# Seven block products of a gated FFN: another product order, earlier reading out of PSUM, and later joins of the transposed blocks

## The chip, the cores and the metric

The kernel runs on one NeuronCore of a Trainium2 chip. The metric is the device time of one execution in microseconds (us), the median of several executions. A profiled execution gives, beside its time, a trace of every instruction on five engines: TensorE (PE, the matmuls; PEld, its weight loads), VectorE (DVE), ScalarE (ACT), GpSimd (POOL) and SyncE (SP, which here only issues transfers).

## The reference

A decoder trunk of two layers on 512 tokens of width 1024. Each layer is a half-step SwiGLU, a mixing block of three attention branches, and a second half-step SwiGLU:

```python
def _swiglu(t, w_gate, w_up, w_down):
    return (jax.nn.silu(t @ w_gate) * (t @ w_up)) @ w_down

for l in range(DEPTH):                                    # DEPTH = 2
    f = _swiglu(_rmsnorm(h, ffn1_pre_g[l]), ffn1_w_gate[l], ffn1_w_up[l], ffn1_w_down[l])
    h = h + 0.5 * _rmsnorm(f, ffn1_post_g[l])
    ...                                                   # mixing block
    f = _swiglu(_rmsnorm(h, ffn2_pre_g[l]), ffn2_w_gate[l], ffn2_w_up[l], ffn2_w_down[l])
    h = h + 0.5 * _rmsnorm(f, ffn2_post_g[l])
```

The FFN is 2816 features wide. All is float32, and the change touches only the four FFNs, which the program names a0, c0, a1, c1 (a: first of a layer, c: second).

## The kernel before

**Three matmuls for one.** TensorE multiplies float32 operands as a sum of a rounded high part and a low part. `split` (L182, L183) makes the pair: ACT casts the source to the high part (wh, uh, ah), DVE subtracts it from the source to get the low part (wl, ul, al). `mm3` then issues three matmuls for one product: high by high (L205), high by low weights (L206), low activations by high weights (L207).

**Seven products for eight.** 2048 of the 2816 features of an FFN go through a Strassen-Winograd scheme: the activations are cut into 2 x 2 blocks (halves of the tokens by halves of the 1024 inputs), the weights into 2 x 2 blocks as well, and seven products of sums of blocks stand for eight block products. A run of seven products handles 1024 features of one matrix. So an FFN has four such groups, in this order: G0 and U0 (gate and up, features 0 to 1023), G1 and U1 (gate and up, features 1024 to 2047). Behind them come 14 products of the down projection, D, in the same manner. The remaining 768 features go as plain products, a pair of 128-feature blocks ahead of G0 and the others between the D products.

**One product.** `token_product(ci, up, n, uns)` issues product n of a group: 24 matmuls of 128x512, over two weight units (k0 = 0 and 2) and two PSUM banks e. The seven products use three pairs of banks: c0 collects products 0, 3, 5 and 6, c1 is a copy of c0 made after product 0 (L747, on ACT) onto which product 1 adds, and c2 collects products 2 and 4. After each product but 0 its sum is read out of PSUM into SBUF while the bank goes on collecting: products 2 and 3 by ACT copies (L775), products 4 and 5 by DVE additions (L777, followed by L784 or L786), products 1 and 6 by ACT silu (L781, gate) or DVE multiplication (L779, up). So product 5 may not write into a bank of c0 before product 3 is read out of it, and product 6 not before product 5 is.

**Order.** `ORDER` is 0, 2, 1, 3, 4, 5, 6 for all four groups. `sums` makes the sums of activation blocks (x00, x11 and the pairs uh/ul of products 2 to 5) in steps spread over the first products of G0. `BlockUnit` loads a raw weight block; for products 2, 3, 5, 6 a DVE subtraction (L327) forms the sum of weight blocks, in a kept tile t or in the raw tile; products 2 and 4 inherit raw tiles of products 0 and 3. The raw tiles come in turn from the pools "raw" (2 buffers) and "o".

**Turning the result.** A product of activations by weights has the tokens on the partitions, and the down projection needs the features there. So each finished up block (after products 1, 4, 5, 6) is transposed by `turn`, called behind the matmuls of each later product: two ACT copies (L800) separate its 16-bit halves, SP issues two DMA transposes (L801), and two products later two ACT copies join the halves (L804). The halves land in an own buffer for products 1 and 5, in short-lived tiles for 4 and 6.

**Who sets the order on an engine.** The code is traced once, and a list scheduler orders the instructions of each engine by priority and by its own cost estimates; parts of the program are pinned to the written order, these groups are not. Each engine then runs its list strictly in order, waiting on semaphores. The loads are issued by SP ahead of their use, within the buffers of the pools.

## Time and profile before

| | us |
|---|---|
| runs | 2379.33, 2377.66, 2384.99 (median 2379.33) |
| profiled execution: its time | 2378.89 |
| profiled execution: span | 2377.2 |
| PE busy | 2348.8 |
| DVE busy | 1805.5 |
| ACT busy | 1515.2 |
| POOL busy | 76.0 |
| mean granted TensorE clock | 0.999 |

The span is the time from the first to the last instruction. Matmuls are pipelined: one 128x512 matmul has about 0.39 us in the trace, but the next starts 0.227 us after it, so that a busy PE can't be taken for a PE at its peak; what is lost there is seen in its waits. A row of the timeline gives start, duration, engine, line, operation, output<-input, shape, and in brackets the idle time of the engine ahead of it with what ended it. In the names, pwa0u is a PSUM bank of FFN a0, group "up"; pda one of the down products; wh_ga and wl_ga weights (gate, FFN of kind a), ula the low part of a sum of activation blocks, hra and sa gate and up results in SBUF.

### The profile page before, as it was taken

The numbers are of one execution on the slowest core, as the hardware profiler recorded it, in microseconds if no ns is written. First come the engines' busy times: TensorE is split into PE (matmuls) and PEld (weight loads), VectorE is DVE, ScalarE is ACT, GpSimd is POOL, SyncE is SP. The second block draws the span as 40 slices with busy tenths as digits, with TensorE's granted clock in tenths as the row PEclk, the third lists the DMA queues.
The fourth block names the chain that finished last, engine by engine and source line by source line (L and its number), as shares of the span: only waits on it lengthen the run. The fifth ranks groups of instructions, "written<-read, shape, count | busy, mean of one in ns | idle before, by whom it ended". The sixth has DMA issues, their size and how long they took to land.

```text
span 2377.2 us, 31155 instructions
## 1 busy us (share of the span) xinstructions
PE 2348.8 (99%) x11719; PEld 1982.8 (83%) x11719; DVE 1805.5 (76%) x2358; ACT 1515.2 (64%) x2306; POOL 76.0 (3%) x134
## 2 busy tenths in 40 slices
PE   9999999999999999999999999999999999999998
PEld 7777889888888888778888878888888888887787
DVE  8876877667777689778788778766777767897785
ACT  6777565577766556775557665655777664666744
POOL 0000000000111000000000000000001100000000
PEclk9999999999999999999999999999999999999999
DMA  5666455223223556664647664532323235576643
GB/s 199 194 176 182 159 190 151 75 81 94 86 75 107 186 178 177 185 186 142 230 134 208 182 177 161 199 110 71 98 72 98 80 116 200 160 203 171 194 145 141
DMA packets 299754, 354.98 MB, mean 149 GB/s; under 512 B 78266, under 2 KB 192978, under 8 KB 299604
## 3 DMA queue, kind: packets, MB, share of 16 engines
q1 hardware_dynamic: 299508, 352.97, 48.3%
q8 instruction: 92, 1.51, 0.3%
q14 instruction: 58, 0.48, 0.1%
q0 software_dynamic: 96, 0.03, 0.0%
HBM read 319.39 MB, written 16.78 MB: 141 GB/s over the span
## 4 chain that ended last, share of the span: by engine, by line
PE 84%; DVE 5%; DMA 5%; ACT 4%; issue 2%; SPq 0%; POOL 0%; DVEq 0%; ACTq 0%
PE pg L206 4%; PE pg L205 4%; PE pg L207 4%; PE pda L206 2%; PE pda L207 2%; PE pdc L206 2%; PE pda L205 2%; PE pdc L207 2%; PE pdc L205 2%; PE pb L207 1%; PE pb L206 1%; PE pb L205 1%; DMA raw_da<-in_ffn_w_down_dram 1%; PE pq L206 1%; PE pq L205 1%
## 5 line engine op out<-in xcount | busy, mean ns | idle before, releaser
L205 PE MATMUL pg<-us_a,wh_wg 128*128 128x512 f32 x384 | 150.9, 393 | 0.0
L207 PE MATMUL pg<-us_a,wl_wg 128*128 128x512 f32 x384 | 149.8, 390 | 0.0
L206 PE MATMUL pg<-us_a,wh_wg 128*128 128x512 f32 x384 | 149.8, 390 | 0.0
L206 PE MATMUL pda<-wl_da,aha 128*128 128x512 f32 x224 | 87.8, 392 | 3.5 <-DVE wl_da L183 3.5
L206 PE MATMUL pdc<-wl_dc,ahc 128*128 128x512 f32 x224 | 87.9, 392 | 3.0 <-DVE wl_dc L183 3.0
L205 PE MATMUL pdc<-wh_dc,ahc 128*128 128x512 f32 x224 | 86.8, 390 | 1.4 <-ACT wh_dc L182 1.3
L205 PE MATMUL pda<-wh_da,aha 128*128 128x512 f32 x224 | 86.7, 390 | 1.1 <-ACT wh_da L182 1.1
L207 PE MATMUL pdc<-wh_dc,alc 128*128 128x512 f32 x224 | 87.2, 389 | 0.0
L207 PE MATMUL pda<-wh_da,ala 128*128 128x512 f32 x224 | 87.2, 389 | 0.0
L183 DVE TENSOR_TENSOR wl_da<-raw_da,wh_da 128x1024 fp32r<-128x1024 f32 x50 | 60.9, 1223 | 34.3 <-ACT wh_da L182 34.3
L207 PEld LDWEIGHTS pg<-us_a,wl_wg 128*128 128x128 f32 x384 | 72.1, 188 | 15.2
L183 DVE TENSOR_TENSOR wl_dc<-raw_dc,wh_dc 128x1024 fp32r<-128x1024 f32 x50 | 61.0, 1222 | 30.5 <-ACT wh_dc L182 30.4
L205 PEld LDWEIGHTS pg<-us_a,wh_wg 128*128 128x128 f32 x384 | 72.1, 188 | 14.1
L206 PEld LDWEIGHTS pg<-us_a,wh_wg 128*128 128x128 f32 x384 | 72.2, 188 | 14.1
L182 ACT CAST wh_da<-raw_da 128x1024 fp32r<-128x1024 f32 x50 | 52.2, 1050 | 47.0 <-PE pda L207 16.6
L182 ACT CAST wh_dc<-raw_dc 128x1024 fp32r<-128x1024 f32 x50 | 52.3, 1050 | 43.5 <-PE pdc L207 17.6
L186 DVE SCALAR_TENSOR_TENSOR wl_wg<-raw_wg,wh_wg 128x1024 fp32r<-128x1024 f32 x48 | 58.4, 1220 | 22.2 <-ACT wh_wg L185 22.2
L200 DVE SCALAR_TENSOR_TENSOR ga<-pg,bgate,ga 128x512 f32<-128x512 f32 x48 | 35.9, 747 | 50.0 <-ACT ga L199 50.0
L185 ACT ACTIVATE wh_wg<-raw_wg 128x1024 fp32r<-128x1024 f32 x48 | 50.6, 1058 | 24.7 <-PE pv L1096 11.7
L183 DVE TENSOR_TENSOR wl_uc<-raw_uc,wh_uc 128x1024 fp32r<-128x1024 f32 x44 | 53.7, 1220 | 16.5 <-ACT wh_uc L182 16.5
L182 ACT CAST wh_uc<-raw_uc 128x1024 fp32r<-128x1024 f32 x44 | 46.1, 1050 | 30.7 <-PE pgc L206 7.6
L183 DVE TENSOR_TENSOR wl_ua<-raw_ua,wh_ua 128x1024 fp32r<-128x1024 f32 x44 | 53.6, 1219 | 15.0 <-ACT wh_ua L182 15.0
(647 smaller groups left out, 8053.7 us busy)
## 6 DMA issues: line engine op xcount, KB each, us to landing
raw_da<-in_ffn_w_down_dram SPq DMA_DIRECT2D x66, 512.0 KB, 4.4
raw_dc<-in_ffn_w_down_dram SPq DMA_DIRECT2D x66, 512.0 KB, 4.2
raw_ga<-in_ffn_w_gate_dram SPq DMA_DIRECT2D x52, 512.0 KB, 4.3
raw_ua<-in_ffn_w_up_dram SPq DMA_DIRECT2D x52, 512.0 KB, 4.4
raw_gc<-in_ffn_w_gate_dram SPq DMA_DIRECT2D x52, 512.0 KB, 4.1
raw_uc<-in_ffn_w_up_dram SPq DMA_DIRECT2D x52, 512.0 KB, 3.6
raw_wg<-in_w_gate_dram SPq DMA_DIRECT2D x48, 512.0 KB, 3.5
raw_wo<-in_w_out_dram SPq DMA_DIRECT2D x24, 512.0 KB, 3.4
```

The lines of the kernel that those rows point to most:

```text
L182: both = [nc.scalar.copy(h_ap, src)]
L183: make = lambda: nc.vector.tensor_tensor(l_ap, src, h_ap.bitcast(F32), ALU.subtract)
L185: both = [nc.scalar.activation(h_ap, src, AF.Copy, scale=scale)]
L186: make = lambda: nc.vector.scalar_tensor_tensor(l_ap, src, scale, h_ap.bitcast(F32), ALU.mult, ALU.subtract)
L200: nc.vector.scalar_tensor_tensor(t, z, minus, t, ALU.max, ALU.add)
L205: nc.tensor.matmul(pt, lh, rh, start=start, stop=False, skip_group_check=free)
L206: nc.tensor.matmul(pt, lh, rl, start=False, stop=False, skip_group_check=free)
L207: nc.tensor.matmul(pt, ll, rh, start=False, stop=stop, skip_group_check=free)
```

## The change

The product order is a table by group: G0, U0 and G1 take 0, 2, 3, 1, 5, 4, 6, and U1 keeps 0, 2, 1, 3, 4, 5, 6. Where the raw tile of a product lies is now a table by product instead of a cycle. The copy of c0 into c1 is issued ahead of product 2 instead of ahead of product 1, and the banks of c1 are taken there too. All reading out of PSUM, of the token products and of the down products, is issued under a higher scheduler priority. The halves of a transposed block lie in the own buffer by the position of its product among the four (first and third), and the join comes two products later for the second of the four and, in U0, the first; for the others it comes three products later. The computation and the number of matmuls (11,348 rows on PE) stay the same.

```diff
-    ORDER = (0, 2, 1, 3, 4, 5, 6)
+    ORDERS = ((0, 2, 3, 1, 5, 4, 6), (0, 2, 1, 3, 4, 5, 6))
+    PLACES = ("raw", "o"), ("raw", "o"), (None, None), ("o", "o"), (None, None), ("raw", "o"), ("raw", "o")
...
-            if n in (0, 1, 2):
-                st["c", n] = [pbank("z" if n == 0 else "mm", f"pw{nm}_{e}") for e in range(2)]
-            if n == 1:
+            for c in {0: (0,), 2: (2, 1)}.get(n, ()):
+                st["c", c] = [pbank("mm" if c else "z", f"pw{nm}_{c}{e}") for e in range(2)]
+            if n == 2:
                 for e in range(2):
+                  with tc.high_priority(offset=300):
                     nc.scalar.copy(st["c", 1][e][:], st["c", 0][e][:])
...
+            with tc.high_priority(offset=300):
+                for e in range(2):
+                    p = pts[e][:].rearrange("p (f q) -> p f q", f=2)
...
             if up and n in (1, 4, 5, 6):
-                turns.append([nm, g, (2 * ci + q[1], q[0]), n in (1, 5), 0, None])
+                at = [n for n in ORDERS[ci] if n in (1, 4, 5, 6)].index(n)
+                turns.append([nm, g, (2 * ci + q[1], q[0]), at % 2 == 0, 0, None, 2 if at == 1 or ci == 0 and at == 0 else 3])
...
-                if kk in (0, 1) and age == 2:
+                if kk in (0, 1) and age == back:
...
-            turns[:] = [one for one in turns if one[4] < 3]
+            turns[:] = [one for one in turns if one[4] <= one[6]]
...
-            places, had = itertools.cycle(("raw", "o", "o")), {}
-            for n in ORDER:
-                uns = [BlockUnit(n, w, ND // 2, k, 2, S, keep, f"{nm}_{n}_{k}", n in (2, 4) or next(places))
+            had, order = {}, ORDERS[ci and up]
+            for n in order:
+                uns = [BlockUnit(n, w, ND // 2, k, 2, S, keep, f"{nm}_{n}_{k}", PLACES[n][k // 2])
...
-                early = ci == 0 and not up and n in ORDER[:4]
+                early = ci == 0 and not up and n in order[:4]
...
         def product(at, uns):
...
+            with tc.high_priority(offset=300):
+                if n == 0:
+                    st["b", 1] = [pbank("z", f"pd{name}_1_{e}") for e in range(2)]
```

In the changed file the lines stand lower by 1 (L716 becomes L717, L719 L720), 2 (L747 becomes L749) or 3 (L777 becomes L780, L784 L787); L182, L183 and L327 keep theirs. In the order lists that follow a row is line, operation, output<-inputs and shape. A weight tile such as wl_gc_0_3_0 is the low part for FFN kind c, gate, group 0, product 3, unit 0, with a buffer number behind it.

The first place is DVE in G0 of c0, from the last splits of product 2's surroundings to the low part ulc_3 that product 3 needs. Before:

```order
L183 TENSOR_TENSOR wl_gc_0_1_0_8083<-raw_gc_0_1_0_7933,wh_gc_0_1_0_8082 128x1024
L183 TENSOR_TENSOR hidc_17_8079<-sc_17_8076,hidc_17_8079 128x512
L716 TENSOR_TENSOR x11c_7997<-x11c_7997,x00c_8036 128x1024
L183 TENSOR_TENSOR wl_gc_0_1_2_8089<-raw_gc_0_1_2_7935,wh_gc_0_1_2_8088 128x1024
L327 TENSOR_TENSOR tgc_0_0_7929<-raw_gc_0_3_0_7937,tgc_0_0_7929 128x1024
L183 TENSOR_TENSOR ulc_3_8104<-x11c_7997,uhc_3_8103 128x1024
```

Now, from the same point of the program:

```order
L327 TENSOR_TENSOR tgc_0_0_7929<-raw_gc_0_3_0_7933,tgc_0_0_7929 128x1024
L183 TENSOR_TENSOR hidc_17_8079<-sc_17_8076,hidc_17_8079 128x512
L327 TENSOR_TENSOR tgc_0_2_7931<-raw_gc_0_3_2_7935,tgc_0_2_7931 128x1024
L183 TENSOR_TENSOR wl_gc_0_3_0_8084<-tgc_0_0_7929,wh_gc_0_3_0_8083 128x1024
L717 TENSOR_TENSOR x11c_7997<-x11c_7997,x00c_8036 128x1024
L183 TENSOR_TENSOR wl_gc_0_3_2_8089<-tgc_0_2_7931,wh_gc_0_3_2_8088 128x1024
L183 TENSOR_TENSOR wl_gc_0_1_0_8124<-raw_gc_0_1_0_7937,wh_gc_0_1_0_8123 128x1024
L183 TENSOR_TENSOR ulc_3_8102<-x11c_7997,uhc_3_8101 128x1024
```

Ahead of ulc_3 DVE now has two operations of 128x1024 more than before, and the product that reads ulc_3 comes one product earlier.

The second place is PE in a0, at the end of G1's product 5 (before) or 4 (now) and the beginning of its product 6, whose weights are wh_ga_1_6. Before:

```order
L207 MATMUL pwa0g_0_1_1135<-wh_ga_1_5_2_1268,ula_5_665 128x512
L205 MATMUL pwa0u_0_0_1430<-wh_ua_1_0_0_1342,us_x_130 128x512
L206 MATMUL pwa0u_0_0_1430<-wl_ua_1_0_0_1343,us_x_130 128x512
L205 MATMUL pwa0g_0_0_1134<-wh_ga_1_6_0_1300,us_x_131 128x512
L206 MATMUL pwa0g_0_0_1134<-wl_ga_1_6_0_1301,us_x_131 128x512
```

Now:

```order
L206 MATMUL pwa0g_2_21_1181<-wl_ga_1_4_2_1265,uha_4_623 128x512
L207 MATMUL pwa0g_2_21_1181<-wh_ga_1_4_2_1264,ula_4_624 128x512
L205 MATMUL pwa0g_0_00_1132<-wh_ga_1_6_0_1298,us_x_131 128x512
L206 MATMUL pwa0g_0_00_1132<-wl_ga_1_6_0_1299,us_x_131 128x512
L207 MATMUL pwa0g_0_00_1132<-wh_ga_1_6_0_1298,us_x_131 128x512
```

Two matmuls of U1's product 0 stood ahead of product 6; they now stand behind it, with the rest of their product.

The third place is DVE at the end of U1 in a0, where the down products begin (wl_da_0_0_0 are the low weights of the first). Before:

```order
L183 TENSOR_TENSOR wl_ua_1_6_2_1589<-tua_1_2_1263,wh_ua_1_6_2_1588 128x1024
L183 TENSOR_TENSOR ala_1_0_1739<-hra_2_1531,aha_1_0_1738 128x1024
L183 TENSOR_TENSOR wl_da_0_0_0_1624<-raw_da_0_0_0_1539,wh_da_0_0_0_1623 128x1024
L777 TENSOR_TENSOR hra_3_1492<-hra_3_1492,pwa0u_0_0_1430 128x2x256
L777 TENSOR_TENSOR hra_3_1492<-hra_3_1492,pwa0u_0_1_1431 128x2x256
```

Now:

```order
L183 TENSOR_TENSOR wl_ua_1_6_2_1593<-tua_1_2_1229,wh_ua_1_6_2_1592 128x1024
L183 TENSOR_TENSOR ala_1_0_1739<-hra_2_1531,aha_1_0_1738 128x1024
L780 TENSOR_TENSOR hra_3_1496<-hra_3_1496,pwa0u_0_00_1430 128x2x256
L183 TENSOR_TENSOR wl_da_0_0_0_1624<-raw_da_0_0_0_1539,wh_da_0_0_0_1623 128x1024
L780 TENSOR_TENSOR hra_3_1496<-hra_3_1496,pwa0u_0_01_1431 128x2x256
```

The reading out of product 5's first bank moved ahead of the split of the first down weights. On PE, four matmuls of the first down product stood ahead of U1's product 6 here; they now stand behind it.

More of the change, by code (lines that the diff above doesn't have):

```diff
@@ L770, in token_product @@
             r = hidden_rows(2 * ci + q[1])[:, :, HALVES[q[0]]] if up else g
-            for e in range(2):
-                p = pts[e][:].rearrange("p (f q) -> p f q", f=2)
-                re, ge = r[:, 2 * e:2 * e + 2], g[:, 2 * e:2 * e + 2]
-                if n in (2, 3):
-                    nc.scalar.copy(re, p)
-                elif n in (4, 5):
-                    nc.vector.tensor_tensor(re, re, p, ALU.add)
-                elif up:
-                    nc.vector.tensor_tensor(ge, p, ge, ALU.mult)
-                else:
-                    nc.scalar.activation(re, p, AF.Silu)
-            if n in (4, 5):
-                if up:
-                    nc.vector.tensor_tensor(g, r, g, ALU.mult)
-                else:
-                    nc.scalar.activation(r, r, AF.Silu)
+            with tc.high_priority(offset=300):
+                for e in range(2):
+                    p = pts[e][:].rearrange("p (f q) -> p f q", f=2)
+                    re, ge = r[:, 2 * e:2 * e + 2], g[:, 2 * e:2 * e + 2]
+                    if n in (2, 3):
+                        nc.scalar.copy(re, p)
+                    elif n in (4, 5):
+                        nc.vector.tensor_tensor(re, re, p, ALU.add)
+                    elif up:
+                        nc.vector.tensor_tensor(ge, p, ge, ALU.mult)
+                    else:
+                        nc.scalar.activation(re, p, AF.Silu)
+                if n in (4, 5):
+                    if up:
+                        nc.vector.tensor_tensor(g, r, g, ALU.mult)
+                    else:
+                        nc.scalar.activation(r, r, AF.Silu)
             if up and n in (1, 4, 5, 6):
-                turns.append([nm, g, (2 * ci + q[1], q[0]), n in (1, 5), 0, None])
+                at = [n for n in ORDERS[ci] if n in (1, 4, 5, 6)].index(n)
+                turns.append([nm, g, (2 * ci + q[1], q[0]), at % 2 == 0, 0, None, 2 if at == 1 or ci == 0 and at == 0 else 3])
         def turn(kk):
             for one in turns:
-                nm, g, (row, i), own, age, planes = one
+                nm, g, (row, i), own, age, planes, back = one
                 if kk == 1 and age == 0:
@@ L874, in product @@
                 return
-            if n == 0:
-                st["b", 1] = [pbank("z", f"pd{name}_1_{e}") for e in range(2)]
-                for e in range(2):
-                    nc.scalar.copy(st["b", 1][e][:], pts[e][:])
-                return
-            i, hf = TO[n]
-            for e in range(2):
-                f = dst.fs[2 * i + e][:, HF[hf]]
-                if n in (4, 5):
-                    nc.vector.tensor_tensor(f, f, pts[e][:], ALU.add)
-                else:
-                    nc.scalar.copy(f, pts[e][:])
+            with tc.high_priority(offset=300):
+                if n == 0:
+                    st["b", 1] = [pbank("z", f"pd{name}_1_{e}") for e in range(2)]
+                    for e in range(2):
+                        nc.scalar.copy(st["b", 1][e][:], pts[e][:])
+                    return
+                i, hf = TO[n]
+                for e in range(2):
+                    f = dst.fs[2 * i + e][:, HF[hf]]
+                    if n in (4, 5):
+                        nc.vector.tensor_tensor(f, f, pts[e][:], ALU.add)
+                    else:
+                        nc.scalar.copy(f, pts[e][:])
         def products():
```

## The prediction

> **What bounds the kernel now.** I read the page's head first, then the list of what PE waits for, then the timeline around each of those waits. The head of the page:

> ```profile
> span 2377.2 us, 31155 instructions
> PE 2348.8 (99%) x11719; PEld 1982.8 (83%) x11719; DVE 1805.5 (76%) x2358; ACT 1515.2 (64%) x2306; POOL 76.0 (3%) x134
> ```

> PE is busy in all but 2377.2 - 2348.8 = 28.4 us. The change keeps every matmul, so it can win no more than idle time of PE, and only that in the FFNs. The view of PE's waits (line that waits, what ended the wait: us in all, times, longest) names it:

> ```profile
> PE pda L206 <- DVE wl_da L183: 3.5, 4, 1.3
> PE pdc L206 <- DVE wl_dc L183: 3.0, 4, 0.8
> PE pwa0u L205 <- ACT wh_ga L182: 2.0, 1, 2.0
> ...
> PE pdc L205 <- ACT wh_dc L182: 1.3, 1, 1.3
> PE pda L205 <- ACT wh_da L182: 1.1, 1, 1.1
> PE pwa0g L207 <- DVE ula L183: 1.1, 1, 1.1
> PE pwc1u L206 <- DVE wl_uc L183: 0.8, 1, 0.8
> PE pwa0u L206 <- DVE wl_ua L183: 0.8, 1, 0.8
> ...
> PE pwa1u L206 <- DVE wl_ua L183: 0.6, 1, 0.6
> ...
> PE pwa0u L205 <- ACT wh_ua L182: 0.5, 1, 0.5
> PE pwc1u L205 <- ACT wh_uc L182: 0.5, 1, 0.5
> ...
> PE pwc0u L206 <- DVE wl_uc L183: 0.4, 1, 0.4
> PE pwc0u L205 <- ACT wh_gc L182: 0.3, 1, 0.3
> ```

> By place these are: the two rows of wh_ga and wh_gc, 2.3 us, at product 6 of U0 (a0 and c0); six rows of ua and uc, 0.8 + 0.8 + 0.6 + 0.5 + 0.5 + 0.4 = 3.6 us, at the first matmuls of U1, which stand ahead of G1's product 6; the four rows of da and dc, 3.5 + 3.0 + 1.3 + 1.1 = 8.9 us, in D; and 1.1 us at G0's product 4 in a0. Together 15.9 us, 0.7% of the time. That is the most that can be won, and it needs all of them to go with nothing new.

> **Term 1, product 6 of U0.** The chain in a0, from the timelines of ACT, DVE and PE:

> ```profile
> 108.97 1.36 ACT L804 COPY hra<-tra0u 128x1024 uint16<-128x1024 uint16 x1 [1.78 <-DMA tra0u<-tha0u]
> 110.21 1.03 ACT L182 CAST wh_ua<-tua 128x1024 fp32r<-128x1024 f32 x1
> 111.27 1.22 DVE L183 TENSOR_TENSOR wl_ua<-tua,wh_ua 128x1024 fp32r<-128x1024 f32 x1 [0.37 <-ACT wh_ua L182]
> 112.42 0.68 DVE L777 TENSOR_TENSOR hra<-hra,pwa0u 128x512 f32<-128x512 f32 x1
> 113.24 0.47 PE L205 MATMUL pwa0u<-wh_ua,us_x 128*128 128x512 f32 x1 [1.97 <-ACT wh_ga L182]
> ```

> ACT stands 1.78 us for the transpose that its join reads; behind the join is queued a cast, behind that on DVE a split, and behind the split the reading out of product 5, for which product 6 waits 1.97 us (the view puts that down to wh_ga, which was cast earlier; L777 ends just ahead of the matmul). With product 4 between 5 and 6 the read has 24 matmuls of 0.227 us, 5.4 us, more to be done in. The whole chain would have to grow by 3.5 us more to be seen again, so I take -2.3 us. The ends: -2.3, and 0 if the joins, which still come two products after products 1 and 5 in U0, hold up ACT by that much more. Nothing is late next there: G1's first weights are needed one product later than the read was.

> **Term 2, start of U1.** The matmuls of U1's product 0 no longer stand ahead of G1's product 6. They now come 24 matmuls, 5.4 us, later, and their longest wait was 0.8, so -3.6 us. G1's product 6 is covered by product 4 as in U0. Instead, one matmul of a later product stands ahead of product 2 in U0, G1 and U1; it waits for its cast where ACT is behind. Such single waits were 0.4 to 0.8 in the rows above; there are eleven such places, ACT has a whole product's time for the cast in each, and I take 0.5 us in all, between 0 and 11 x 0.4 = 4.4.

> **Term 3, start of D.** The order keeps 5 straight ahead of 6 in U1. So where PE used to wait on the first down matmuls, it now waits for the reading out of product 5:

> ```profile
> 192.26 1.22 DVE L183 TENSOR_TENSOR ala<-hra,aha 128x1024 fp32r<-128x1024 f32 x1
> 193.47 1.23 DVE L183 TENSOR_TENSOR wl_da<-raw_da,wh_da 128x1024 fp32r<-128x1024 f32 x1
> 193.49 0.49 PE L205 MATMUL pda<-wh_da,aha 128*128 128x512 f32 x1 [1.12 <-ACT wh_da L182]
> 194.75 0.50 PE L206 MATMUL pda<-wl_da,aha 128*128 128x512 f32 x1 [0.77 <-DVE wl_da L183]
> ...
> 1367.66 1.22 DVE L183 TENSOR_TENSOR ala<-hra,aha 128x1024 fp32r<-128x1024 f32 x1
> 1370.48 0.50 PE L206 MATMUL pda<-wl_da,aha 128*128 128x512 f32 x1 [0.75 <-DVE wl_da L183]
> ```

> In a0 PE ends product 5 at 193.49 - 1.12 = 192.37 and loses 1.12 + 0.77 = 1.89 us. Now the first read stands behind ala, which ends at about 193.4; with 0.68 for the read product 6 starts at 194.1, and PE loses 1.7. That wins 0.2. In a1 PE is through with product 5 at about 1370.48 - 0.75 - 0.23 = 1369.5, and the read ends at 1367.66 + 1.14 + 0.68 = 1369.5: 0.75 becomes about 0.2, for the second bank. With c0 like a0 (its two waits are 1.3 and 0.8) and c1 like a1, 0.2 + 0.3 + 0.55 + 0.55 = -1.6 us. The ends: -5.4 (all that D's first matmuls lose: 1.1 + 1.3 and four times 0.75) and +2, if the read comes 0.5 later in each. Of the 8.9 us in D the other 3.5 stand at later weights, which the change leaves where they are; 0.

> **Term 4, G0.** This is the price of the order. DVE has no free time there:

> ```profile
> 882.00:914.60 32.60, 32.60 (x146) 27.01 (x145) 32.47 (x32) 21.30 (x26) 0.00 (x0) 1.00 0.54 172
> ```

> (PE, PEld, DVE, ACT, POOL busy, granted clock, share of the DMA engines, GB/s): DVE is busy 32.47 of 32.60 us, since beside the splits it makes the sums of activations. In c0:

> ```profile
> 885.27 0.68 DVE L627 TENSOR_TENSOR sc<-puc,sc 128x512 f32<-128x512 f32 x1
> 887.71 1.06 ACT L182 CAST wh_gc<-raw_gc 128x1024 fp32r<-128x1024 f32 x1 [1.10 <-DMA raw_gc<-in_ffn_w_gate_dram]
> 890.10 1.22 DVE L327 TENSOR_TENSOR tgc<-raw_gc,tgc 128x1024 f32<-128x1024 f32 x1
> 891.23 1.22 DVE L183 TENSOR_TENSOR ulc<-x11c,uhc 128x1024 fp32r<-128x1024 f32 x1
> 892.91 0.39 PE L205 MATMUL pwc0g<-wh_gc,us_b 128*128 128x512 f32 x1
> ```

> An operation of 128x1024 starts 1.14 us after the one ahead (890.10 to 891.23). PE ends product 2 at 892.91; then came product 1, which reads activations that were there from the start, and now comes product 3, which reads ulc (the row at 891.23). Following the new list from L627 at 885.27: a weight sum, a split of 128x512, the second weight sum not before its raw tile has landed (I take 887.7, when the load that stood in this place landed), then split, sum L717, split, split, and ulc at 887.7 + 5 x 1.14 = 893.4, done by 894.6. PE has five matmuls that don't need it, to 892.91 + 5 x 0.227 = 894.0. So it stands 0.6. The tenth operation behind is the low part for product 5: 893.4 + 10 x 1.14 = 904.8, done 906.0; PE reaches product 5 after two products and the 0.6 at 904.4, has four matmuls for it, to 905.3, and stands 0.7. Products 4 and 6 find theirs ready. 1.3 us in each of c0, a1, c1, where the groups look alike; in a0, where product 4 waited for its low part before, the same lateness at three products comes to 2.6, less the 1.1 that stood there: 1.5. Sum +5.4 us. The ends: 0 if the load lands earlier (its tile now is in "o", where a buffer is free before one in "raw" is), and the second rival's price.

> **At nothing.** The copy of c0 into c1 is the same two ACT copies a product earlier; PE needs them at product 3 or 1 only, and ACT is busy 21.30 of 32.60 us in G0. The reads in D are unchanged in kind and were waited for nowhere in the list above. Joins three products later have left the wait for the transpose behind, at 5.4 us each; the loads and transposes on SP are the same in number and keep their order among themselves, but stand behind waits for other buffers, which no row prices; that uncertainty is in term 4's ends.

> **Sum.** -2.3 - 3.6 + 0.5 - 1.6 + 5.4 = -1.6 us. Against the profiled execution's own 2378.89 that is 2377.3, and I forecast 2377; the median of the runs, 2379.33, stands 0.4 above the profiled one. A measurement of this kernel can tell about 0.3%, 7.1 us, from no change (its three runs lie 7.3 apart): the forecast is within.

> **Rivals.** (a) Slower: product 3's raw tiles in G0 land no earlier than their use at 890.10 before. Then ulc is seven operations from there, 890.10 + 6 x 1.14 = 896.9, done 898.1, and PE stands 898.1 - 894.0 = 4.1 in each of four groups: 16.4 in place of 5.4, so 2377.3 + 11 = 2388. It decides from a landing at about 889.5, since each us of lateness there costs 4. For it: the row at 887.71 shows a load in this place that was waited for 1.10 us, and DVE has no slack to make up with. Against it: the loads are issued in order of use, and product 3 has moved up.

> (b) Faster: the named waits at U0, U1 and the start of D go wholly, and G0's lateness is taken up by PE's reordering: -2.3 - 3.6 - 5.4 = -11.3, so 2367.6. For it: the read is put ahead of the split of wl_da. Against it: ala stands ahead of both, and DVE in G0 is full.

> (c) The change does not do what it says: the waits only move (product 6 of U0 and the start of U1 wait for the same late casts one product on), and G0 still pays. Then terms 3 and 4 with 1 for the single matmuls remain, -1.6 + 5.4 + 1 = +4.8, so 2384. Against it: both places get 5 us of other matmuls, more than any wait shown.

> (d) New short stalls of PE bring its granted clock down. The stretch with the most idle time in the trace does not show it:

> ```profile
> 190.00:198.00 8.00, 6.12 (x26) 4.50 (x25) 8.00 (x8) 8.00 (x9) 0.00 (x0) 1.00 0.49 99
> ```

> PE is busy 6.12 of 8.00 us there and the granted clock is 1.00. If the four G0 groups ran at half pace, each window of 32.6 us would take as much again, 130 us in all, 2507. [...]

> **How the numbers follow.** The forecast 0.54, (a) 0.18, (b) 0.13, (c) 0.14, (d) 0.01. The likeliest one's own range goes from 2373 (term 4 at 1) to 2382 (term 4 at 8, single waits at 2). (b) is left out below 2368 in half its cases; (a) reaches a little over 2388, so 2368 to 2389 leaves out some 0.17. Faster by over 0.3%, under 2372.2: most of (b) and the edge of the forecast, 0.17. Slower by over 0.3%, over 2386.5: (a), (d) and a fifth of (c) and of the forecast's upper edge, 0.25. Within: 0.58.

> **What would show it.** Right: no wait at U0's product 6 and none of pwa0u, pwc0u, pwa1u, pwc1u on U1's first weights; at U1's product 6 a wait that ends with L780, 1.7 us in a0 and c0 and under 0.3 in a1 and c1; in G0 two waits of L207 on ula or ulc, 0.6 and 0.7, with DVE full. Wrong: G0 waits of 3 us and more, ended by a transfer on DVE's or ACT's side (a); no wait in G0 at all (b); waits of the same sum at other matmuls of U0 and U1 (c). The prediction fails altogether if the reads, put first, make DVE or ACT stand for PE in D, where I counted nothing.

## The result, and the profile after

The change makes the kernel slower: 2400.5 us median (2394.89 to 2401.6, 4 runs) against 2382.16 (2377.66 to 2386.56, 4 runs) of the kernel before, a ratio of 1.0077 with a 95% interval of 1.0063 to 1.0091. The forecast was 2377, in a range from 2368 to 2389; 2400.5 lies outside it. The profiled execution took 2399.88 us, 21.0 more than that of before. The head of the page after:

```profile
span 2398.2 us, 31131 instructions
PE 2356.6 (98%) x11719; PEld 1990.3 (83%) x11719; DVE 1806.5 (75%) x2358; ACT 1516.1 (63%) x2306; POOL 73.4 (3%) x134
```

Two things have grown. PE stands 2398.2 - 2356.6 = 41.6 us, 13.2 more than before; and the same matmuls (x11719 in both heads) keep it busy for 7.8 us more (2356.6 against 2348.8). What it waits for now (line, what ended the wait: us in all, times, longest):

```profile
PE pwa0g L205 <- ACT pwa0g L749: 5.3, 1, 5.3
PE pwa1g L205 <- ACT pwa1g L749: 3.3, 1, 3.3
PE pda L206 <- DVE wl_da L183: 2.9, 1, 2.9
PE pdc L206 <- DVE wl_dc L183: 2.8, 2, 2.3
PE pwc0u L205 <- DVE hrc L780: 2.3, 1, 2.3
PE pwa1u L205 <- DVE hra L780: 2.1, 1, 2.1
PE pwc1g L205 <- ACT pwc1g L749: 2.0, 1, 2.0
PE pwa0g L205 <- ACT uha L182: 1.9, 2, 1.7
PE pwc0g L205 <- ACT pwc0g L749: 1.8, 1, 1.8
...
PE pwa1g L207 <- DVE ula L183: 1.2, 2, 0.9
PE pwc0g L207 <- DVE ulc L183: 1.2, 2, 0.8
PE pwc1g L207 <- DVE ulc L183: 1.2, 2, 0.8
PE pwc1u L205 <- DVE hrc L780: 1.2, 1, 1.2
PE pwa0u L205 <- DVE hra L780: 1.0, 1, 1.0
```

The waits at product 6 of U0 and at the start of U1 are gone. New are four waits for the copies of c0 into c1 (L749), 5.3 + 3.3 + 2.0 + 1.8 = 12.4 us, all four in G1; and four for the reads of product 5 (L780) ahead of product 6 of U1, 6.6 us. The first of them, in a0, from the timelines of PE and ACT:

```profile
123.02 0.39 PE L207 MATMUL pwa0g<-wh_ga,us_x 128*128 128x512 f32 x1
124.09 1.03 ACT L182 CAST wh_ga<-tga 128x1024 fp32r<-128x1024 f32 x1
125.02 1.33 ACT L808 COPY hra<-tra0u 128x1024 uint16<-128x1024 uint16 x1
126.22 1.03 ACT L804 COPY tha0u<-sa 128x1024 uint16<-128x1024 uint16 x1
127.16 1.04 ACT L182 CAST wh_ga<-tga 128x1024 fp32r<-128x1024 f32 x1
128.10 0.58 ACT L749 COPY pwa0g<-pwa0g 128x512 f32<-128x512 f32 x1
128.73 1.22 PE L205 MATMUL pwa0g<-wh_ga,uha 128*128 128x512 f32 x2 [5.33 <-ACT pwa0g L749]
```

The row at 123.02 is the last matmul of G1's product 0. Next in PE's list is one matmul of product 3, ahead of all of product 2. It writes into c0, so the copy of that bank has to be done, and it reads weights whose cast is the row at 127.16. ACT is not idle from here on: it works through a cast, a join and a half of a transposed block, and only then comes to these two. PE stands 5.33 us, with the 24 matmuls of product 2 behind the one.

Behind such waits PE runs slower: behind the one in a0 the matmuls start 0.43 us apart (130.18 to 130.61), from 132.20 on 0.23. The first window of 4 us inside the FFNs with a clock under 1.00 (PE, PEld, DVE, ACT, POOL busy, granted clock, share of the DMA engines, GB/s):

```profile
128.00:132.00 4.00, 3.27 (x8) 2.59 (x9) 3.77 (x4) 4.00 (x6) 0.00 (x0) 0.58 0.66 123
```

The granted clock was 0.58 of full speed over the 4 us in which the wait in a0 ends. There are seven such places in the FFNs, with a lowest window of 0.56 to 0.70 each: the four waits for L749, two of those for L780 (c0, a1) and one in D. In the trace of before there is one, at 2168 us.

The mean granted clock differs between executions of one kernel, so one trace alone could mislead. The four executions of the changed kernel had a mean granted clock of 0.993 to 0.996, 0.994 on average; the 65 executions of the kernel before that ran beside the experiments had 0.994 to 1.000, 0.997 on average. The lower clock belongs to the change, then, and not to the one profiled execution.

### The profile page after: what moved, and what is told of

Read it like the earlier page. It is cut to its first block, busy times and chain, and to the rows that moved or that the text cites. A ratio compares the mean times of both kernels' runs of the same rounds, so it can differ in the third digit from the quotient of the medians.

```text
span 2398.2 us, 31131 instructions
## 1 busy us (share of the span) xinstructions
PE 2356.6 (98%) x11719; PEld 1990.3 (83%) x11719; DVE 1806.5 (75%) x2358; ACT 1516.1 (63%) x2306; POOL 73.4 (3%) x134
## 4 chain that ended last, share of the span: by engine, by line
PE 84%; DVE 5%; DMA 4%; ACT 3%; issue 3%; SPq 0%; POOL 0%; DVEq 0%; ACTq 0%
PE pg L206 4%; PE pg L205 4%; PE pg L207 4%; PE pda L206 3%; PE pda L207 3%; PE pda L205 3%; PE pdc L206 3%; PE pdc L207 3%; PE pdc L205 3%; PE pb L205 1%; PE pb L207 1%; PE pb L206 1%; PE pq L206 1%; PE pq L205 1%; PE pk L206 1%
## 5 line engine op out<-in xcount | busy, mean ns | idle before, releaser
L205 PE MATMUL pg<-us_a,wh_wg 128*128 128x512 f32 x384 | 150.9, 393 | 0.0
L206 PE MATMUL pg<-us_a,wh_wg 128*128 128x512 f32 x384 | 149.7, 390 | 0.0
L207 PE MATMUL pg<-us_a,wl_wg 128*128 128x512 f32 x384 | 149.7, 390 | 0.0
L206 PE MATMUL pda<-wl_da,aha 128*128 128x512 f32 x224 | 88.4, 395 | 2.9 <-DVE wl_da L183 2.9
L206 PE MATMUL pdc<-wl_dc,ahc 128*128 128x512 f32 x224 | 87.6, 391 | 2.8 <-DVE wl_dc L183 2.8
L207 PE MATMUL pda<-wh_da,ala 128*128 128x512 f32 x224 | 87.9, 392 | 0.0
L207 PE MATMUL pdc<-wh_dc,alc 128*128 128x512 f32 x224 | 87.2, 389 | 0.0
L205 PE MATMUL pda<-wh_da,aha 128*128 128x512 f32 x224 | 86.8, 391 | 0.0
L205 PE MATMUL pdc<-wh_dc,ahc 128*128 128x512 f32 x224 | 86.5, 389 | 0.0
L207 PEld LDWEIGHTS pg<-us_a,wl_wg 128*128 128x128 f32 x384 | 72.1, 188 | 15.1
L206 PEld LDWEIGHTS pg<-us_a,wh_wg 128*128 128x128 f32 x384 | 72.2, 188 | 14.1
L205 PEld LDWEIGHTS pg<-us_a,wh_wg 128*128 128x128 f32 x384 | 72.1, 188 | 14.1
L183 DVE TENSOR_TENSOR wl_da<-raw_da,wh_da 128x1024 fp32r<-128x1024 f32 x50 | 60.9, 1223 | 30.0 <-ACT wh_da L182 29.6
L183 DVE TENSOR_TENSOR wl_dc<-raw_dc,wh_dc 128x1024 fp32r<-128x1024 f32 x50 | 61.0, 1223 | 28.4 <-ACT wh_dc L182 28.0
L182 ACT CAST wh_da<-raw_da 128x1024 fp32r<-128x1024 f32 x50 | 52.2, 1050 | 44.9 <-PE pda L207 19.7
L182 ACT CAST wh_dc<-raw_dc 128x1024 fp32r<-128x1024 f32 x50 | 52.3, 1049 | 43.4 <-PE pdc L207 18.3
L182 ACT CAST wh_uc<-raw_uc 128x1024 fp32r<-128x1024 f32 x44 | 46.4, 1054 | 33.6 <-issue 7.7
L183 DVE TENSOR_TENSOR wl_ga<-raw_ga,wh_ga 128x1024 fp32r<-128x1024 f32 x40 | 48.1, 1221 | 23.6 <-ACT wh_ga L182 23.6
L183 DVE TENSOR_TENSOR wl_uc<-raw_uc,wh_uc 128x1024 fp32r<-128x1024 f32 x44 | 53.4, 1222 | 16.4 <-ACT wh_uc L182 16.2
```

The source lines that it names most:

```text
L182: both = [nc.scalar.copy(h_ap, src)]
L183: make = lambda: nc.vector.tensor_tensor(l_ap, src, h_ap.bitcast(F32), ALU.subtract)
L205: nc.tensor.matmul(pt, lh, rh, start=start, stop=False, skip_group_check=free)
L206: nc.tensor.matmul(pt, lh, rl, start=False, stop=False, skip_group_check=free)
L207: nc.tensor.matmul(pt, ll, rh, start=False, stop=stop, skip_group_check=free)
```

## The experiments

All kernels below compute the whole reference. Ratios are to the kernel before, with 95% intervals, each from runs beside it on one chip; the changed kernel's is 1.0077.

**1. Product 2 first on PE.** The changed kernel, with one order added: the matmuls of the product behind product 2 (3, or 1 in U1) may not stand ahead of product 2's last.

```diff
+                        if n in (1, 3) and "last2" in st:
+                            for i in own:
+                                tc.add_manual_dep(i, st["last2"], NOSYNC, reason="after product 2")
```

> The changed kernel, with one added order on PE: in every group no matmul of the product behind product 2 may stand ahead of product 2. Theory 1 (the single matmul of product 3 that stands ahead of product 2 in G1 waits for the copies L749, and the whole of product 2 waits behind it): the 12.5 us of waits that end with L749 fall to under 2 us, the stretches of lower clock behind them go too, and the time falls by 14 to 20 us to about 2382 to 2386. Theory 2 (the copies come late on ACT because of the late joins, and product 3 has to wait for them in any case): the waits only move behind product 2 and lose what product 2 covers, 5.4 us at most in a0 and less elsewhere; the time falls by under 8 us. Theory 3 (putting the reads first is what costs): no change by this edit in the waits for L780, 6.6 us, under either.

Measured: 2388.1 us, ratio 1.0030 (1.0018 to 1.0043), 12.4 less than the changed kernel, and 11 less by the two ratios. PE's row at the head of the page:

```profile
PE 2349.4 (98%) x11719; PEld 1983.4 (83%) x11719; DVE 1803.6 (76%) x2358; ACT 1511.6 (63%) x2306; POOL 73.5 (3%) x134
```

The window of G1 in a0 whose clock was 0.58:

```profile
128.00:132.00 4.00, 3.84 (x17) 2.83 (x17) 3.58 (x4) 4.00 (x6) 0.00 (x0) 1.00 0.69 129
```

And the longest of its waits:

```profile
PE pda L206 <- DVE wl_da L183: 6.1, 2, 3.5
PE pdc L206 <- DVE wl_dc L183: 3.2, 2, 2.3
PE pwc0u L205 <- DVE hrc L791: 2.9, 1, 2.9
```

No wait for the copy is left, product 2 covers it; in its place stand 2.1 us for low weights, nearly all in a0. PE's busy time is back at 2349.4, and the clock in that window at 1.00; two places with a lower clock are left in the FFNs. So the single matmul cost 12.4 us of standing and most of the 7.2 us of slower matmuls. The profiled span fell by 11.3 us and not by the 19.6 that these two make, because other waits grew: by those 2.1 us, in D from 5.7 to 9.3, and for the reads in U1 (L791 here) from 6.6 to 9.0, together 8.1. Theory 1 holds as to the cause; its 14 to 20 us were missed by what came back in these waits.

**2. All joins two products later, as before.** The matmuls stand in the same order on PE as in the changed kernel.

```diff
-                turns.append([nm, g, (2 * ci + q[1], q[0]), at % 2 == 0, 0, None, 2 if at == 1 or ci == 0 and at == 0 else 3])
+                turns.append([nm, g, (2 * ci + q[1], q[0]), at % 2 == 0, 0, None, 2])
```

> The changed kernel, with every join two products later as before; its matmuls stand in the same order on PE as in the changed kernel. Theory 1 (the single matmul): it still stands there, so waits for L749 stay at over half of 12.5 us, and the time within 6 us of the changed kernel. Theory 2 (late joins crowd ACT at the start of G1): the waits for L749 fall under 4 us and the time by 10 us or more. On the waits for L780 at product 6 of U1 (6.6 us): if the join that waits for its transpose is what delays ala, they change by more than 2 us; if not, they stay within 1.

Measured: 2395.53 us, ratio 1.0053 (1.0035 to 1.0070). Its longest waits for the copy:

```profile
PE pwa0g L205 <- ACT pwa0g L749: 4.8, 1, 4.8
PE pwa1g L205 <- ACT pwa1g L749: 3.2, 1, 3.2
```

With 1.8 in c0 and 1.3 in c1, 11.1 of 12.4 us are still there, so the late joins are not what makes the copies late. The waits for L780 sum to 6.9 us, as good as unchanged; but the join ahead of ahc in c0 still stands 3.66 us for its transpose (3.97 in the changed kernel), so the edit did not take that join's wait away and says nothing on whether it delays ala and alc. The time is 5 us lower, and the intervals overlap; a small price of the late joins is likely and not shown.

**3. Everything at ordinary priority.** The scheduler's higher priority is taken from the reads and the copies.

```diff
-            with tc.high_priority(offset=300):
+            if True:
```

> The changed kernel, with all its reading out of PSUM and the copies L749 issued at ordinary priority. The scheduler then puts the single matmul of product 3 ahead of product 2 in G1 only in a0, and five such matmuls in U0 of c0, a1 and c1; in U1 four-matmul pieces of product 6 are gone. Theory 1: the waits for L749 in G1 stay in a0 (some 5 us) and go in c0, a1 and c1 (7.2 us), unless the five matmuls in U0 wait too; the time falls by 7 to 12 us. Theory 3 (the reads put first cost): the waits for L780 at product 6 of U1 go or halve, and the time falls by over 6 us on that account. Theory 2: no change in the joins, so the waits for the copies stay near 12 us and the time within 4 us of the changed kernel.

Measured: 2416.19 us, ratio 1.0143 (1.0123 to 1.0162), 16 us slower than the changed kernel. Its costliest waits:

```profile
PE pda L206 <- DVE wl_da L183: 10.5, 4, 4.3
PE pdc L206 <- DVE wl_dc L183: 8.5, 4, 3.2
PE pwa0g L205 <- ACT pwa0g L749: 4.8, 1, 4.8
```

The wait for L749 is 4.8 us in a0 and at most 0.3 elsewhere, just where the single matmul still stands in the list and where not, as theory 1 has it. The waits for L780 at product 6 of U1 are gone, as theory 3 has it. Yet the sum went the other way: D waits 19.0 us instead of 5.7, reads in gate groups come late (6.1 us), and so do low up weights (7.4 us in c0, a1 and c1). These last are the early matmul again, at another place: in U1 of all four FFNs five matmuls of product 1 now stand ahead of product 2, where the changed kernel has one (the expectation speaks of U0). In c0 the second of the five and the first matmul of product 2 (uhc), from the timeline of PE:

```profile
1017.97 0.50 PE L206 MATMUL pwc0u<-wl_uc,us_b 128*128 128x512 f32 x1 [2.97 <-DVE wl_uc L183]
1019.07 0.63 PE L205 MATMUL pwc0u<-wh_uc,uhc 128*128 128x512 f32 x1
```

Taking the priority away reorders PE's list as well, so the 16 us are the net of several changes, and no run separates them. In this order the priority is a gain, not the cost; theory 3 falls for the sum, and my expectation of a shorter time with it.

**4. Both of the first two edits.**

> Both edits: product 2 first on PE and every join two products later. If the filler is the cause and the joins are not (theory 1), this is within 3 us of the first kernel of this call. If both matter (theories 1 and 2), it is faster than either by 3 us or more. Left in both cases: about 5 us in G0 (two waits of 0.8 and 0.4 us in c0, a1, c1, 1.9 in a0) and the waits for L780 in U1. Estimate 2382.

Measured: 2386.53 us, ratio 1.0023 (1.0011 to 1.0034), within 3 us of experiment 1, as theory 1 has it; the estimate of 2382 was missed by 4.5. Still 8.8 us of waits for the reads in U1, and 6.9 in D.

**5. U1 in the new order too**, on top of experiment 4.

```diff
-    ORDERS = ((0, 2, 3, 1, 5, 4, 6), (0, 2, 1, 3, 4, 5, 6))
+    ORDERS = ((0, 2, 3, 1, 5, 4, 6), (0, 2, 3, 1, 5, 4, 6))
```

> Product 2 first on PE, every join two products later, and U1 too in the order 0, 2, 3, 1, 5, 4, 6, so that product 4 stands between 5 and 6 there as well. Against the kernel of the last call without that last edit (2386.5 us; waits for the reads ahead of product 6 of U1 2.5 + 2.1 + 2.7 + 1.5 = 8.8 us): theory A (product 6 of U1 waits only because product 5 comes straight ahead of it): those 8.8 us go, and the time falls by 7 to 10 us, to about 2378. Theory B (ACT is late there because of its joins, and whatever comes next waits): the waits move to the first down matmuls or to products 5 and 4 of U1, and the time falls by under 3 us.

Measured: 2390.25 us, ratio 1.0021 (1.0010 to 1.0032), no faster than experiment 4. Theory A is right about the place, for no wait for a read is left at product 6 of U1; about the time theory B is right, which had under 3 us. The waits moved, though not to the first down matmuls: D now waits 14.0 us for casts of down weights, four times, 7.2 us in a0 and a1, 6.8 in c0 and c1, in a0 from 220.2 to 224.3 us, where D begins at 198.3. With that PE's idle time in the profiled executions is 1.1 us less than in experiment 4; its busy time is 6.7 us more (2353.5 against 2346.8), at a mean granted clock of 0.995 against 0.997.

**6. G0 as before, the other three new**, else as experiment 5.

```diff
-    ORDERS = ((0, 2, 3, 1, 5, 4, 6), (0, 2, 3, 1, 5, 4, 6))
+    ORDERS = ((0, 2, 1, 3, 4, 5, 6), (0, 2, 3, 1, 5, 4, 6))
...
-            had, order = {}, ORDERS[ci and up]
+            had, order = {}, ORDERS[bool(ci or up)]
```

> As the kernel above, but G0 keeps the order 0, 2, 1, 3, 4, 5, 6 of before; U0, G1 and U1 have the new one. If the two operations more on DVE ahead of product 3 are what costs in G0: its waits, 1.2 us in each of c0, a1 and c1 and 1.9 in a0, go back to 1.1 in a0 alone, and this is 4 to 5 us faster than the kernel above. If theory A holds too, what is left of PE's waits is D's, 7 to 9 us, and the time is about 2373, 0.3% under before: faster than both. By theory B about 2381.

Measured: 2383.95 us, ratio 1.0001 (0.9991 to 1.0012). Against experiment 5 that is 0.2% less, the 4 to 5 us that G0's waits were said to cost, and of these waits 0.7 us is left. The forecast of 2373 failed, as D waits here too:

```profile
PE pda L205 <- ACT wh_da L182: 7.8, 2, 4.6
PE pdc L205 <- ACT wh_dc L182: 5.8, 2, 4.0
```

The one in a0, from the timelines of ACT and PE:

```profile
222.43 1.04 ACT L182 CAST aha<-asa 128x1024 fp32r<-128x1024 f32 x1 [3.11 <-DVE asa L853]
223.39 1.99 ACT L182 CAST wh_da<-raw_da 128x1024 fp32r<-128x1024 f32 x2
224.48 1.22 PE L205 MATMUL pda<-wh_da,aha 128*128 128x512 f32 x2 [4.59 <-ACT wh_da L182]
```

Ahead of the cast that PE waits for, ACT stands 3.11 us for a sum of hidden blocks (asa), which DVE makes. That is the order of two casts in ACT's list. Both lists have a part in asa's lateness. The join ahead of it on ACT starts at 216.39, after 2.07 us of standing for its transpose; DVE stands 4.55 us for the cast behind that join, and from 218.86 on it makes a low part (ala) and a sum of weights before it comes to asa at 221.19. Which of the two would be enough alone is not tested.

**7. The kernel before, with the priority alone**: the reads and the copy of c0 (before product 1, as it was) under the higher priority, with order, joins and places as before.

> The kernel before, with nothing of the change but the higher priority of the reading out of PSUM and of the copy of c0 (order, joins, places as before). Theory 3 (the priority by itself costs, since DVE and ACT then stand for PE ahead of splits): slower than before by 0.3% or more. If it is of use, as the run without it suggests (16 us slower than the changed kernel): within 0.2% of before or faster, the waits at product 6 of U0 (2.7 us) smaller, and at product 6 of U1 waits for the reads of 4 to 9 us in place of those of the first down matmuls, 5.4.

Measured: 2388.31 us, ratio 1.0023 (1.0010 to 1.0035): slower by 0.2%, between the two expectations. The waits for the first down matmuls (5.4 us) have gone, and at product 6 of U1 reads are waited for instead, 6.3 us. Product 6 of U0 waits 2.7 us as before, where less was expected. The later waits in D grew from 3.5 to 8.3 us, and these 4.8 us are most of the loss. So it is the priority that turns the one wait at the end of U1 into the other, it makes D wait longer further on, and on the order of before it is a small loss.

**8. The copy in G1 on DVE**, in the changed kernel; PE's list is the changed kernel's.

```diff
-                    nc.scalar.copy(st["c", 1][e][:], st["c", 0][e][:])
+                    copy = nc.vector.tensor_copy if ci == 1 and not up else nc.scalar.copy
+                    copy(st["c", 1][e][:], st["c", 0][e][:])
```

> The changed kernel, with the two copies of c0 into c1 in G1 made by DVE instead of ACT; the matmuls stand in the same order on PE, the single matmul of product 3 ahead of product 2 included. If the copy comes late because of what stands ahead of it in ACT's queue (joins, halves of transposed blocks, casts), the waits for L749, 12.5 us, fall to under 4 us with the single matmul still in its place, and the time falls by 8 to 16 us, to about 2386 to 2391. If the copy is late for another reason (product 0's banks, or whatever engine makes it), the waits stay over 8 us and the time within 4 us of the changed kernel.

Measured: 2397.58 us, ratio 1.0054 (1.0037 to 1.0070), not the 8 to 16 us less. No wait for the copy is left, but the same matmul waits for its other condition:

```profile
PE pwa0g L205 <- ACT wh_ga L182: 4.2, 1, 4.2
PE pwa1g L205 <- ACT wh_ga L182: 3.0, 1, 3.0
```

In a0 the cast and the first of the copies, from the timelines of ACT and DVE:

```profile
126.41 1.04 ACT L182 CAST wh_ga<-tga 128x1024 fp32r<-128x1024 f32 x1
126.68 0.69 DVE L750 COPY pwa0g<-pwa0g 128x512 f32<-128x512 f32 x1
```

With c0 and c1 these waits are 4.2 + 3.0 + 1.8 + 1.6 = 10.6 us of 12.4, and D waits 11.2 us instead of 5.7. The copy was the last of two things that stood side by side in ACT's list; the cast ends at 127.45 here, and DVE is through with the copy at 127.37, hardly sooner, as its own list stood 0.99 us for a cast of ACT not long before. Together with experiment 1 this says that the cause is a matmul that comes a product too early, not the copy.

**9. Only U0 and G1 new**, with product 2 first and joins two products later.

```diff
-    ORDERS = ((0, 2, 3, 1, 5, 4, 6), (0, 2, 1, 3, 4, 5, 6))
+    ORDERS = ((0, 2, 1, 3, 4, 5, 6), (0, 2, 3, 1, 5, 4, 6))
...
-            had, order = {}, ORDERS[ci and up]
+            had, order = {}, ORDERS[ci != up]
```

> Product 2 first on PE, every join two products later, high priority kept; the new order in U0 and G1 alone, G0 and U1 as before. Against the kernel with G0 in the new order too (ratio 1.0023 to before): if G0's waits are a price of its own, 4 to 5 us less, so about 0.2% less, a ratio near 1.000. Left are the waits ahead of product 6 of U1, 7 to 9 us, and D's. Not faster than before by more than 0.1%, if what U1's end and D's loads take in the one place they give back in the other.

Measured: 2382.74 us, ratio 0.9990 (0.9978 to 1.0002). That is the lowest ratio of all and not to be told from before: none of these kernels is shown to be faster. Against experiment 4 the old order in G0 is worth 0.3%. It keeps 9.7 us of waits for reads at U1's product 6.

## Why the prediction was wrong

**Term 1, product 6 of U0: right.** No wait is left there (2.3 us before by the prediction's two rows, 2.7 with two rows for L777), in any kernel with the new order in U0 and the priority. The priority alone did not do it (experiment 7).

**Term 2, start of U1: half right, and the step that failed.** The 3.6 us went. What was mis-sized is the "one matmul of a later product" ahead of product 2, for which I took 0.5 us in all, with 4.4 at most. It measured 12.4 us of standing, all in G1, and most of 7.2 us of slower matmuls; experiment 1 takes both away. I had read the prices 0.4 to 0.8 from matmuls that stood ahead of G1's product 6 before, where their casts were nearly through. The words "ACT has a whole product's time for the cast in each" are what the row at 127.16 refutes: G1's product 0 ends at 123.4 and that cast at 128.2. The copy of c0 was put at nothing, with the words "PE needs them at product 3 or 1 only"; but the matmul that stands ahead of product 2 is one of product 3, so PE needs the copy there too (128.68 in a0). The wait has the length of ACT's arrears, 1.8 to 5.3 us, at the point where the last blocks of U0 are turned and joined beside G1's casts. In U0 and U1 the same single matmul found ACT in time and cost nothing that the view lists.

**Term 3, start of D: the mechanism right, the size wrong.** As forecast, the waits for the first down weights, 5.4 us, gave way to waits that end with L780. They came to 2.3 in c0, 2.1 in a1, 1.2 in c1 and 1.0 in a0, 6.6 instead of about 3.8. In c0, from the timelines of ACT, DVE and PE:

```profile
1037.79 1.36 ACT L808 COPY hrc<-trc0u 128x1024 uint16<-128x1024 uint16 x1 [3.97 <-DMA trc0u<-thc0u]
1039.94 1.04 ACT L182 CAST ahc<-hrc 128x1024 fp32r<-128x1024 f32 x1
1041.22 1.22 DVE L183 TENSOR_TENSOR alc<-hrc,ahc 128x1024 fp32r<-128x1024 f32 x1
1042.36 0.68 DVE L780 TENSOR_TENSOR hrc<-hrc,pwc0u 128x512 f32<-128x512 f32 x1
1043.18 0.58 PE L205 MATMUL pwc0u<-wh_uc,us_b 128*128 128x512 f32 x1 [2.30 <-DVE hrc L780]
```

I had the list right (alc ahead of the read), but took alc's time from before. It stands behind a cast, and the cast, with another between, behind a join that waited 3.97 us for its transpose. This chain is read from the trace; no run takes the join's wait away. The later waits of D, for which I put 0, went from 3.5 to 5.7 us; experiment 7 has more of that with the priority alone.

**Term 4, G0: right.** 1.3 us was forecast for each of c0, a1 and c1, as two waits of L207 on the low parts of products 3 and 5. In c0 they are:

```profile
901.29 0.51 PE L207 MATMUL pwc0g<-wh_gc,ulc 128*128 128x512 f32 x1 [0.82 <-DVE ulc L183]
912.65 0.50 PE L207 MATMUL pwc0g<-wh_gc,ulc 128*128 128x512 f32 x1 [0.41 <-DVE ulc L183]
```

0.82 + 0.41 = 1.23 us, and 1.2 in the other two. In a0 it is 1.9, for uha, where 2.6 was forecast. Experiments 6 and 9, with G0 alone put back, show it as a price of its own, 0.2 to 0.3%.

**Priority: nothing was put for it, and it is large.** In this order the kernel without it is 16 us slower (experiment 3; 7.4 us of waits there are those of early matmuls), on the old one it costs 0.2% (experiment 7).

**The rivals.** (a) did not happen, the loads for product 3 were in time. (b) and (c) did not either. (d), the falling clock, got 0.01 and was part of the result: 7.8 us of PE's busy time. I dismissed it on one window, 1.88 us of idle time in 8 at a clock of 1.00. It was not the stretch with the most idle time (PE is busy 5.94 of the first 8 us), and the trace of before held a case against me, behind two waits of 0.50 and 0.76 us at U1's first weights in c1:

```profile
2168.00:2172.00 4.00, 3.14 (x7) 2.11 (x8) 3.49 (x4) 1.91 (x2) 0.00 (x0) 0.74 0.82 247
```

The trace after has seven such places in the FFNs, behind waits of 1.83 to 5.33 us. What was mis-priced there is the size, too: not whole groups at half speed, but 3.41 us at a time, once 6.83.

**The sum.** The changes of the waits: +12.4 (single matmul), +6.6 - 5.4 + 2.2 (end of U1, D), +4.4 (G0, 1.9 + 3 x 1.2 less 1.1), -2.3 (U0) and -3.6 (U1) make +14.3, where PE's idle time grew by 13.2; the 1.1 between them is not taken apart. The 13.2 and the 7.8 of slower matmuls make the 21.0.

## What to carry to other kernels

An engine that works its list in order pays for one early instruction with everything queued behind it (in a0 PE stood 5.33 us for one matmul, with the 24 of product 2 behind it): when a scheduler puts a single matmul of a later product ahead of a whole one, price it by the arrears of the engine that feeds it at that place, not by what such matmuls waited elsewhere. A wait that is taken away at one hand-over (a read, a first weight) is worth only what the next one leaves: experiments 5 and 6 cleared U1 and lost nearly as much in D. And a wait on TensorE can cost more than its length: behind seven waits of 1.83 to 5.33 us in the trace after the granted clock was 0.50 for 3.41 us or more, so the clock behind the waits belongs in the sum.

## What the runs showed of the hardware

```profile
125.22:128.63 3.41, 0.00 (x0) 0.00 (x0) 3.41 (x4) 3.41 (x5) 0.00 (x0) 1.00 0.22 46
128.63:132.04 3.41, 3.31 (x8) 2.63 (x9) 3.19 (x4) 3.41 (x5) 0.00 (x0) 0.50 0.74 138
971.72:975.13 3.41, 1.58 (x7) 1.21 (x7) 3.41 (x4) 3.41 (x6) 0.00 (x0) 1.00 0.41 77
975.13:978.54 3.41, 3.41 (x9) 2.64 (x9) 1.96 (x2) 3.41 (x4) 0.00 (x0) 0.50 0.67 82
60.37:63.78 3.41, 1.80 (x8) 1.15 (x7) 3.41 (x4) 2.04 (x2) 0.00 (x0) 1.00 0.58 175
```

All falls of one trace start whole multiples of 3.4133 us apart: in the trace after 975.13 - 128.63 = 846.5 = 248 x 3.4133, in that of before 2374.70 (behind PE's last matmul) - 2169.90 = 204.8 = 60 x 3.4133. A window is from here on one of these steps, counted on from the falls of its trace. Six of the seven falls in the FFNs last one window, which lacks 1.7 us of full speed; the one in a1 at 1316.46 lasts two, with PE busy 2.17 us of its first. So behind the waits of 5.33 us (a0) and of 1.83 us (c0) the clock was low for the same 3.41 us.

In these two traces the falls go with the idle time within one window, not with the length of the wait. The 1.83 us of c0 lie whole in the window from 971.72. The 1.71 us in G0 of a0 (at 63.89) lie in the window from 60.37, all but 0.1, and no fall followed; the 2.33 us in D of c1 (at 2260.20) are split over two windows, with PE busy 2.74 and 1.76 us, and were followed by none. I counted the windows of both traces, from 28 us to PE's last matmul: of those at full clock in which PE stood 1.9 us or more, 6 of 6 were followed by half clock; with 1.6 to 1.9 us it was 1 of 5; with less it was one alone, that of 1.36 us in the trace of before. Why the ones between differ the traces do not show. The first fall comes 2.43 us behind a whole multiple of 3.4133 in the trace of before, 2.33 in that after, and in experiment 9, by the clock of 0.84 over 192 to 196 us, about 0.2. That a wait of some 2 us costs the clock or not partly by chance is my estimate from these places and the two waits above.
